# Two of a pair's weight sums by adding transfers, in six groups of a hybrid attention and convolution block

## The chip, the cores and the metric

The kernel runs on one core of a Trainium2 chip. The metric is the time of one execution on the device in microseconds (us); the number that counts is the median of several runs.

The core has five engines that work side by side and wait for each other by semaphores: PE (TensorE, the matrix engine, with its weight loads shown as PEld), DVE (VectorE), ACT (ScalarE), POOL (GpSimd) and SP (SyncE, which here only issues transfers). Sixteen DMA engines move data between the chip's main memory and the on-chip memory. A transfer is issued from the queue of an engine, here SP's and, for a few small ones, ACT's (q1 and q10 in the profile).

## The reference

One layer over 256 tokens of width 4096, all in float32:

```
xn   = rms_norm(x)
proj = xn @ w_in                 # 4096 x 14336: q, k, v, z_a, a_c, g_c, z_c, each 2048 wide
y_a  = rms_norm(chunked_attention(q, k, v, rel_table)) * silu(z_a)      # 16 heads of 128
y_c  = rms_norm(conv_module(a_c, g_c)) * silu(z_c)
h    = x + concat(y_a, y_c) @ w_out                                      # 4096 x 4096
gate = sigmoid(rms_norm(h) @ w_ple_gate + b)                             # 4096 x 4096
out  = rms_norm(h + gate * (p @ w_ple))
```

The conv module is `a * sigmoid(g)`, a causal depthwise convolution of 31 taps, a layer norm, a swish and a 2048 x 2048 product. Nearly all the work is in the products with the weights, which are read once each from main memory.

## The kernel before

**Products.** The 256 tokens are two halves of 128 rows. A weight tile is 128 rows of a weight matrix by two blocks of 512 columns (`two_columns`, L99; 512 KB). PE multiplies float32 numbers that are split in a high and a low part, so that each 128 x 128 by 128 x 512 product takes three matmuls (high by high, low by high, high by low; `add`, L365). To make the parts of a weight tile, `parts_of` (L199) has ACT write a rounded copy (L204, `wh`) and DVE subtract it from the tile (L205, `wl`).

**Pairs.** `mixed_product` (L327) makes two column blocks of a product at once. It goes over pairs of 128-row blocks of the contracted dimension, 16 pairs for 4096 rows, in an order that is written out by hand (L318 to L325). A pair is done in one of two ways. A plain pair makes the 8 block products as they are, 24 matmuls. A pair with a star is a seven: a Strassen-like scheme that makes 7 block products of sums, 21 matmuls. The sums on the side of the inputs (`comb`) are made once. Those on the side of the weights are made for each such pair, from its two weight tiles w0 and w1 (L421 to L432): `ua` holds w0[0] + w0[1] and w0[1] + w1[1], `ub` holds ua[0] + w1[1] and that plus w1[0]. These are four DVE additions of 128 x 512 (L426, L427, L430, L431), and `ua` and `ub` are split in their parts as the weight tiles are (`pair_parts`, L308; `uh`, `ul`). A seven so takes less of PE and more of DVE and ACT.

Four of the seven products go to PSUM banks of their own (the helpers P1, P5, P6, P7; L418), which are taken from the pool `ps_tmp` at a group's first seven and are read back after its last one (`on_helpers`, L455). Transposes and the attention use the same four banks.

**Groups.** In the first half of the kernel the calls of `mixed_product` through `scaled_pair` (L478) are eight groups: `glu_conv` (L689) for the pairs of column blocks a_c and g_c, c = 0 to 3, and `heads` (L883) for q and k, g = 0 to 3. They run as glu 0, glu 1, heads 0, glu 2, heads 1, glu 3, heads 2, heads 3. Each `heads` is followed by the product for v (`product`, L224) and by the attention of its four heads. Glu 0 has the order `first`, glu 3 the order `early_six` with six sevens, and the other six groups the order `early` with four sevens two apart:

```
early = units("1 3 5 7 0* 9 2* 11 4* 13 6* 15 8 10 12 14")
early_fills = (4, 6, 7, 1, 5, 1, 5, 1, 5, 1, 2, 4, 6, 6, 6, 4)
```

The convolution is work for DVE that is laid between the pairs: each group of `glu_conv` puts 124 taps (L671) into a queue (`later`), and after the n-th pair `fill` (L182) takes the n-th number of `early_fills` out of it. In heads 3 the layer norm and swish stand in that queue, four pieces after each pair.

**Buffers and order.** Weight tiles come from a pool with five buffers (`wpool`, tag w), their high and low parts from three each, `ua` and `ub` together from two (`upool`, tag u), `uh` and `ul` from two each. All loads of weight tiles are issued by SP (L403); a load waits until DVE has freed its buffer. The order of each engine's instructions is set when the program is made, by a planner that goes by program order, by the buffers and by its own estimates of durations; on the chip each engine goes through its list in that order and waits where something is late. Some places are pinned to program order. POOL has 19 instructions, among them the one memset of a part of each attention bias (L895), and issues no transfer.

Of the kernel before, what the change touches and what calls it, by code (L numbers as in the profile page):

```python
# [25 lines left out]
def hybrid_block(  # L26
# [23 lines left out]
    nc = tc.nc  # L50
# [32 lines left out]
    upool = pool("upool", 2, first_sums)  # L83
# [228 lines left out]

    def units(text):

        return [(int(u.rstrip("*")), u.endswith("*")) for u in text.split()]


    dense = units("1 0* 3 2* 5 4* 6* 7 8* 9 10* 11 12* 14* 13 15")  # L318
    first = units("0 1 3 5 7 9 11 13 15 2* 8 4* 10 6* 12 14")
    early = units("1 3 5 7 0* 9 2* 11 4* 13 6* 15 8 10 12 14")  # L320
    early_six = units("1 3 5 7 0* 9 2* 11 4* 13 6* 15 8* 10* 12 14")

    early_fills = (4, 6, 7, 1, 5, 1, 5, 1, 5, 1, 2, 4, 6, 6, 6, 4)
    final = units("1 0* 3 2* 5 4* 6* 7 8* 9 10* 12* 11 13 14 15")
    late = units("1 3 5 7 9 11 13 15 0* 2 4* 6 8* 10* 12 14")  # L325

    def mixed_product(  # L327
        w, col, lhs, comb, order, on_helpers, ahead=None, fills=(0,), on_begin=None, apart=NB,
# [53 lines left out]
        def add_plain(n, k, wh, wl, **kw):  # L382
            pair = order[n][0]
            for j in range(2):
                for h in range(NH):
                    name = (("P2", "P3"), ("P4", "X"))[h][j]
                    add(name, block(2 * pair + k, h), (wh[:, j], wl[:, j]), n, k == 1, **kw)

        done, after = 0, ExitStack()
        if begin:  # L390
            done, behind = begin(add_plain)
# [3 lines left out]
        for n, (pair, seven) in enumerate(order):  # L395
            if n < done:
                continue
            if ahead:
                ahead(pair)
            wts = []  # L400
            for k in range(2):
                wt = wpool.tile([P, 2, NB], F32, tag="w", name="wt")
                nc.sync.dma_start(wt, two_columns(w, 2 * pair + k, col, apart))  # L403
                wts.append(wt)
            if n >= len(order) - n_left:
                for k in range(2):
                    tiles = left[2 * (n - len(order) + n_left) + k]
                    held.append((2 * pair + k, parts_of(wts[k], 2, tiles and tiles())[0]))
                fill(fills[n % len(fills)])
                continue  # L410
            if not seven:
                for k in range(2):
                    add_plain(n, k, *parts_of(wts[k], 2)[0])
                fill(fills[n % len(fills)])
                continue
            begins = not helper
            if begins:
                for name in ("P1", "P5", "P7", "P6"):  # L418
                    helper[name] = ps_tmp.tile([P, NB], F32, tag="tmp", name=f"acc_{name}")
                banks.update(helper)  # L420
            w0, w1 = wts  # L421
            ua = upool.tile([P, 2, NB], F32, tag="u", name="ua")
            ub = upool.tile([P, 2, NB], F32, tag="u", name="ub")
            plus = partial(nc.vector.tensor_tensor, op=ALU.add)
            w0h, w0l = parts_of(w0, 1)[0]
            plus(ua[:, 0], w0[:, 0], w0[:, 1])  # L426
            plus(ua[:, 1], w0[:, 1], w1[:, 1])  # L427
            uah, ual = pair_parts(ua)
            w1h, w1l = parts_of(w1, 2)[0]
            plus(ub[:, 0], ua[:, 0], w1[:, 1])  # L430
            plus(ub[:, 1], ub[:, 0], w1[:, 0])  # L431
# [12 lines left out]
            add("P3", s_of(3), (w1h[:, 1], w1l[:, 1]), n, True)  # L444
            add("P6", s_of(2), (ubh[:, 0], ubl[:, 0]), n, True)
            add("P4", block(k1, 1), (ubh[:, 1], ubl[:, 1]), n, True)
            if begins and on_begin:
                on_begin()
            if begins:
                tc.add_manual_dep(  # L450
                    made[first].ins, last_transpose[0].ins.name,
                    mybir.DependencyInfo(mybir.DependencyClass.NoSync, mybir.DependencyReason.DATA),
                    reason="transposes before the helpers take their banks",
                )
            if n == last_seven:  # L455
                on_helpers(helper)
            fill(fills[n % len(fills)])
# [61 lines left out]
    r_x = cpool.tile([P, NH], F32, name="r_x")  # L519
# [169 lines left out]
    def glu_conv(c):  # L689
        if c == 0:  # L690
            sg, gate = scaled_pair(
                w_in0, o_a, o_g - o_a, first, r_x, (1,), begin=first_pairs
            )
        else:
            last = c == CW // NB - 1
            sg, gate = scaled_pair(
                w_in0, o_a + c * NB, o_g - o_a, early_six if last else early, r_x, early_fills,
                ahead=more_combinations if last else None,
            )
        for h in range(NH):  # L700
            nc.scalar.activation(gate[:, h, :], gate[:, h, :], AF.Sigmoid)
            tt(sg[:, h, :], sg[:, h, :], gate[:, h, :], ALU.mult)
        uT = spool.tile([P, 4, T], F32, tag="hd", name="uT", bufs=5)
        for pair in range(2):
            pt = tmp_psum()
            for i in range(2):
                for h in range(NH):
                    b = 2 * pair + i
                    nc.tensor.transpose(
                        pt[:, i * T + h * P : i * T + (h + 1) * P],  # L710
                        sg[:, h, b * P : (b + 1) * P],
                        ident,
                    )
# [557 lines left out]
```

## Time and profile before

| | |
|---|---|
| median of 3 runs | 2037.13 us (2036.65 to 2038.36) |
| the profiled execution | 2039.1 us |
| its span, from first to last instruction | 2037.3 us |
| matmuls of PE | 9106 |
| granted clock of PE, mean | 0.998 |
| read from main memory | 406.39 MB, 202 GB/s over the span |
| stretch of the six groups | about 99 to 859 us of the span |

The profile gives for each engine how long it was busy and what ended its idle time. A row of the groups of instructions names the line, the engine, the operation and the tiles (out<-in), how many there were, their busy time and mean duration, and the idle time just before them with what ended it. A row of the waits names who waited for whom, the total, the times and the longest. A row of the stretches has for each engine the busy time and, in brackets, the count of its instructions, then the granted clock, the busy share of the DMA engines and the rate. "Landing" is the time from the issue of a transfer to its last byte.

### The profile page before, as it was taken

Reading aid. Unit: us, or ns where it says so; the run is one execution under the profiler, and the core shown is the slowest. Engines: PE = TensorE matmul, PEld = TensorE weight load, DVE = VectorE, ACT = ScalarE, POOL = GpSimd, SP = SyncE. Lnnn points to the kernel's source line nnn. Section 1 sums busy time; section 2 is a strip of 40 time slices with the busy share of each in tenths; the row PEclk is TensorE's granted clock in tenths of the full one; section 3 lists DMA queues with packets and bytes.
Section 4 is the critical chain, followed back from the end, with each engine's and each line's share of the span. In section 5 each row is a group of like instructions: output and inputs, shape, how many; then the busy total and the mean of one; then the engine's idle time right before and its main releaser. Section 6 shows DMA issues by size and latency. Waiting matters only on the chain.

```text
span 2037.3 us, 26041 instructions
## 1 busy us (share of the span) xinstructions
PE 2019.6 (99%) x9106; PEld 1659.5 (81%) x9106; DVE 1887.9 (93%) x2688; ACT 1200.8 (59%) x1559; POOL 8.1 (0%) x19
## 2 busy tenths in 40 slices
PE   9999999999999999999999999999999999999997
PEld 7888888877888888888888888888888888888876
DVE  7999999799989998868899999999999999999998
ACT  7655546554565546676555656676565666655555
POOL 0000000000000000000000000000000000000000
PEclk9999999999999999999999999999999999999999
DMA  8666665666656665655666666676666656666765
GB/s 295 188 200 204 204 187 165 202 191 189 184 185 204 201 188 183 186 184 199 190 216 204 197 216 199 219 238 204 214 201 205 214 185 208 198 221 205 235 208 179
DMA packets 161853, 412.29 MB, mean 202 GB/s; under 512 B 12974, under 2 KB 16190, under 8 KB 161722
## 3 DMA queue, kind: packets, MB, share of 16 engines
q1 hardware_dynamic: 161072, 409.80, 63.3%
q8 instruction: 71, 1.16, 0.2%
q10 hardware_dynamic: 650, 0.84, 0.1%
q14 instruction: 60, 0.49, 0.1%
HBM read 406.39 MB, written 4.19 MB: 202 GB/s over the span
## 4 chain that ended last, share of the span: by engine, by line
PE 86%; DVE 10%; issue 2%; DMA 1%; ACT 1%; POOLq 0%; POOL 0%; ACTq 0%; DVEq 0%
PE acc L370 61%; PE acc_P L370 15%; PE acc L218 7%; DVE wl L205 4%; DVE cv L677 3%; DMA wt<-in_w_in_dram 1%; PE tmp_ps L170 1%; DVE ul L205 1%; PE tmp_ps L867 0%; PE tmp_ps L849 0%; ACT wh L204 0%; PE acc L358 0%; PE tmp_ps L834 0%; DVE z L492 0%; PE tmp_ps L872 0%
## 5 line engine op out<-in xcount | busy, mean ns | idle before, releaser
L370 PE MATMUL acc<-wh,big_t 128*128 128x512 f32 x3788 | 1172.1, 391 | 0.6 <-DVE z L988 0.3
L204 ACT CAST wh<-wt 128x1024 fp32r<-128x1024 f32 (+1 forms) x737 | 715.8, 982 | 543.0 <-PE acc L370 330.6
L205 DVE TENSOR_TENSOR wl<-wt,wh 128x1024 fp32r<-128x1024 f32 (+1 forms) x737 | 825.4, 1132 | 65.0 <-ACT wh L204 60.1
L370 PEld LDWEIGHTS acc<-wh,big_t 128*128 128x128 f32 x3788 | 708.4, 188 | 146.5 <-issue 0.6
L370 PE MATMUL acc<-wl,big_t 128*128 128x512 f32 x1894 | 731.1, 391 | 1.0 <-DVE wl L205 1.0
L370 PEld LDWEIGHTS acc<-wl,big_t 128*128 128x128 f32 x1894 | 355.2, 188 | 76.7 <-DVE wl L205 3.1
L677 DVE SCALAR_TENSOR_TENSOR cv<-uT,dw,cv 128x255 f32<-128x255 f32 (+23 forms) x480 | 204.9, 467 | 1.1
L204 ACT CAST uh<-ub 128x1024 fp32r<-128x1024 f32 x122 | 128.5, 1054 | 126.2 <-DVE ub L431 102.7
L218 PE MATMUL acc<-wh,big_t 128*128 128x512 f32 x560 | 173.1, 390 | 0.0
L204 ACT CAST uh<-ua 128x1024 fp32r<-128x1024 f32 x122 | 128.7, 1055 | 71.7 <-DVE ua L427 63.5
L205 DVE TENSOR_TENSOR ul<-ub,uh 128x1024 fp32r<-128x1024 f32 x122 | 149.0, 1221 | 8.8 <-ACT uh L204 7.8
L370 PE MATMUL acc_P<-uh,big_t 128*128 128x512 f32 x504 | 154.4, 392 | 0.0
L205 DVE TENSOR_TENSOR ul<-ua,uh 128x1024 fp32r<-128x1024 f32 x122 | 148.9, 1220 | 0.4 <-ACT uh L204 0.2
L218 PEld LDWEIGHTS acc<-wh,big_t 128*128 128x128 f32 x560 | 104.8, 188 | 21.4
L370 PEld LDWEIGHTS acc_P<-uh,big_t 128*128 128x128 f32 x504 | 93.3, 188 | 22.2 <-ACT uh L204 3.7
L218 PE MATMUL acc<-wl,big_t 128*128 128x512 f32 x280 | 109.1, 390 | 0.0
L426 DVE TENSOR_TENSOR ua<-wt 128x512 f32<-128x512 f32 x122 | 83.9, 688 | 25.9 <-DMA wt<-in_w_in_dram 19.0
L370 PE MATMUL acc_P<-ul,big_t 128*128 128x512 f32 x252 | 96.8, 392 | 0.0
L427 DVE TENSOR_TENSOR ua<-wt 128x512 f32<-128x512 f32 x122 | 83.7, 686 | 3.9 <-DMA wt<-in_w_in_dram 3.0
L431 DVE TENSOR_TENSOR ub<-ub,wt 128x512 f32<-128x512 f32 x122 | 83.8, 687 | 1.0
L430 DVE TENSOR_TENSOR ub<-ua,wt 128x512 f32<-128x512 f32 x122 | 83.7, 686 | 0.3
L370 PE MATMUL acc<-uh,big_t 128*128 128x512 f32 x244 | 75.4, 390 | 0.0
(241 smaller groups left out, 1523.0 us busy)
## 6 DMA issues: line engine op xcount, KB each, us to landing
wt<-in_w_in_dram SPq DMA_DIRECT2D x447, 512.0 KB, 4.0
wt<-in_w_out_dram SPq DMA_DIRECT2D x128, 512.0 KB, 4.2
wt<-in_w_ple_gate_dram SPq DMA_DIRECT2D x128, 512.0 KB, 4.2
wt<-in_w_pw_dram SPq DMA_DIRECT2D x32, 512.0 KB, 4.5
hc<-in_x_dram SPq DMA_DIRECT2D x8, 512.0 KB, 5.8
wt<-in_w_ple_dram SPq DMA_DIRECT2D x8, 512.0 KB, 4.2
xin<-in_x_dram SPq DMA_DIRECT2D x7, 512.0 KB, 8.2
out_dram<-hc SPq DMA_DIRECT2D x12, 256.0 KB, 2.4
```

The lines of the kernel that those rows point to most:

```text
L170: nc.tensor.transpose(pt[:, i * T + h * P : i * T + (h + 1) * P], src[:, h, b * P : (b + 1) * P], ident,)
L204: nc.scalar.copy(wh[:, :kc, :], wt[:, :kc, :]),
L205: nc.vector.tensor_tensor(wl[:, :kc, :], wt[:, :kc, :], wh[:, :kc, :].bitcast(F32), ALU.subtract),
L218: nc.tensor.matmul(acc, a, b[:, k, :], start=kb == 0 and kind == 0, stop=kb == kblocks - 1 and kind == 2,)
L370: nc.tensor.matmul(banks[name], a, b, start=name not in begun, stop=final and ends[name] == n and kind == 2 and not (left and name in "P2 ...
L426: plus(ua[:, 0], w0[:, 0], w0[:, 1])
L427: plus(ua[:, 1], w0[:, 1], w1[:, 1])
L430: plus(ub[:, 0], ua[:, 0], w1[:, 1])
L431: plus(ub[:, 1], ub[:, 0], w1[:, 0])
L677: nc.vector.scalar_tensor_tensor(cv[:, i, PAD - k :], uT[:, i, : T + k - PAD], dw[:, b, k : k + 1], cv[:, i, PAD - k :], ALU.mult, ALU.add,)
```

## The change

In the order `early`, and only there, the four sevens get a plus in place of the star and stand three apart in place of two: units 3, 6, 9 and 12 in place of 4, 6, 8 and 10. The numbers of taps laid between are set anew, with the same total of 64; glu 3 keeps its order and the old numbers under a new name.

For a pair with a plus the two sums in `ua` are made by transfers. A new function, `sums_ahead`, is called right after the weight tiles of a unit n are asked for, and for each plus unit among n, n + 1 and n + 2 that has none yet it takes a tile of tag u and issues two transfers of 512 KB: SP loads the column block w0[1] into both halves, and POOL then adds w0[0] to the first half and w1[1] to the second. DVE's additions at L426 and L427 fall away for these pairs. As w0[1] is needed for nothing else, the first weight tile of such a pair is loaded with one column block, 256 KB. `ub` is no tile of its own any more; the two additions left write over `ua`, once its parts are made.

```diff
-    early = units("1 3 5 7 0* 9 2* 11 4* 13 6* 15 8 10 12 14")
+    early = units("1 3 5 0+ 7 9 2+ 11 13 4+ 15 8 6+ 10 12 14")
...
-    early_fills = (4, 6, 7, 1, 5, 1, 5, 1, 5, 1, 2, 4, 6, 6, 6, 4)
+    early_fills = (5, 6, 1, 5, 6, 1, 5, 6, 1, 5, 6, 1, 2, 5, 5, 4)
+    six_fills = (4, 6, 7, 1, 5, 1, 5, 1, 5, 1, 2, 4, 6, 6, 6, 4)
...
+        sums = {}
+
+        def sums_ahead(n):
+            for m in range(n, min(n + 3, len(order))):
+                if order[m][1] != "+" or m in sums:
+                    continue
+                ua = sums[m] = upool.tile([P, 2, NB], F32, tag="u", name="ua")
+                rows = w[2 * order[m][0] * P : (2 * order[m][0] + 1) * P, :]
+                step = P * rows.ap[0][0]
+
+                def columns(first, step):
+                    return bass.AP(
+                        tensor=rows.tensor, offset=rows.offset + first,
+                        ap=[list(rows.ap[0]), [step, 2], [1, NB]],
+                    )
+
+                nc.sync.dma_start(ua, columns(col + apart, 0))
+                nc.gpsimd.dma_start(ua, columns(col, step + apart), accum_op=ALU.add)
...
-                nc.sync.dma_start(wt, two_columns(w, 2 * pair + k, col, apart))
+                if seven == "+" and k == 0:
+                    nc.sync.dma_start(wt[:, 0], w[2 * pair * P : (2 * pair + 1) * P, col : col + NB])
+                else:
+                    nc.sync.dma_start(wt, two_columns(w, 2 * pair + k, col, apart))
                 wts.append(wt)
+            sums_ahead(n)
...
             w0h, w0l = parts_of(w0, 1)[0]
-            plus(ua[:, 0], w0[:, 0], w0[:, 1])
-            plus(ua[:, 1], w0[:, 1], w1[:, 1])
+            if seven == "+":
+                ua = ub = sums[n]
+            else:
+                ua = upool.tile([P, 2, NB], F32, tag="u", name="ua")
+                plus(ua[:, 0], w0[:, 0], w0[:, 1])
+                plus(ua[:, 1], w0[:, 1], w1[:, 1])
             uah, ual = pair_parts(ua)
             w1h, w1l = parts_of(w1, 2)[0]
+            if seven != "+":
+                ub = upool.tile([P, 2, NB], F32, tag="u", name="ub")
             plus(ub[:, 0], ua[:, 0], w1[:, 1])
             plus(ub[:, 1], ub[:, 0], w1[:, 0])
```

More of the change, by code (lines that the diff above doesn't have):

```diff
@@ L313, in units @@
     def units(text):
-        return [(int(u.rstrip("*")), u.endswith("*")) for u in text.split()]
+        return [(int(u.rstrip("*+")), u[-1] if u[-1] in "*+" else "") for u in text.split()]
     dense = units("1 0* 3 2* 5 4* 6* 7 8* 9 10* 11 12* 14* 13 15")
     first = units("0 1 3 5 7 9 11 13 15 2* 8 4* 10 6* 12 14")
-    early = units("1 3 5 7 0* 9 2* 11 4* 13 6* 15 8 10 12 14")
+    early = units("1 3 5 0+ 7 9 2+ 11 13 4+ 15 8 6+ 10 12 14")
     early_six = units("1 3 5 7 0* 9 2* 11 4* 13 6* 15 8* 10* 12 14")
-    early_fills = (4, 6, 7, 1, 5, 1, 5, 1, 5, 1, 2, 4, 6, 6, 6, 4)
+    early_fills = (5, 6, 1, 5, 6, 1, 5, 6, 1, 5, 6, 1, 2, 5, 5, 4)
+    six_fills = (4, 6, 7, 1, 5, 1, 5, 1, 5, 1, 2, 4, 6, 6, 6, 4)
     final = units("1 0* 3 2* 5 4* 6* 7 8* 9 10* 12* 11 13 14 15")
@@ L421, in mixed_product @@
             w0, w1 = wts
-            ua = upool.tile([P, 2, NB], F32, tag="u", name="ua")
-            ub = upool.tile([P, 2, NB], F32, tag="u", name="ub")
             plus = partial(nc.vector.tensor_tensor, op=ALU.add)
             w0h, w0l = parts_of(w0, 1)[0]
-            plus(ua[:, 0], w0[:, 0], w0[:, 1])
-            plus(ua[:, 1], w0[:, 1], w1[:, 1])
+            if seven == "+":
[4 more added lines that the diff above has]
+                plus(ua[:, 1], w0[:, 1], w1[:, 1])
             uah, ual = pair_parts(ua)
             w1h, w1l = parts_of(w1, 2)[0]
+            if seven != "+":
+                ub = upool.tile([P, 2, NB], F32, tag="u", name="ub")
             plus(ub[:, 0], ua[:, 0], w1[:, 1])
@@ L696, in glu_conv @@
             sg, gate = scaled_pair(
-                w_in0, o_a + c * NB, o_g - o_a, early_six if last else early, r_x, early_fills,
+                w_in0, o_a + c * NB, o_g - o_a, *((early_six, r_x, six_fills) if last else (early, r_x, early_fills)),
                 ahead=more_combinations if last else None,
```

## The prediction

> **What bounds the kernel now.** I read the busy shares and the chain on the page first, then the stretches of the six groups that the diff touches, then what waits in them.
>
> ```profile
> span 2037.3 us, 26041 instructions
> ...
> PE 2019.6 (99%) x9106; PEld 1659.5 (81%) x9106; DVE 1887.9 (93%) x2688; ACT 1200.8 (59%) x1559; POOL 8.1 (0%) x19
> ...
> DMA  8666665666656665655666666676666656666765
> GB/s 295 188 200 204 204 187 165 202 191 189 184 185 204 201 188 183 186 184 199 190 216 204 197 216 199 219 238 204 214 201 205 214 185 208 198 221 205 235 208 179
> ...
> PE 86%; DVE 10%; issue 2%; DMA 1%; ACT 1%; POOLq 0%; POOL 0%; ACTq 0%; DVEq 0%
> ...
> L426 DVE TENSOR_TENSOR ua<-wt 128x512 f32<-128x512 f32 x122 | 83.9, 688 | 25.9 <-DMA wt<-in_w_in_dram 19.0
> ...
> L427 DVE TENSOR_TENSOR ua<-wt 128x512 f32<-128x512 f32 x122 | 83.7, 686 | 3.9 <-DMA wt<-in_w_in_dram 3.0
> ...
> wt<-in_w_in_dram SPq DMA_DIRECT2D x447, 512.0 KB, 4.0
> ```
>
> PE is busy 99% of the span and holds 86% of the chain. A busy share can hide slow matmuls, so I checked the pace where PE is fed without a break: in the chain of waits, a stretch of 192 matmuls takes 43.55 us.
>
> ```profile
> 499.47 43.55 PE acc L218 x192
> ```
>
> That is 0.2268 us each. An early group is 12 plain pairs of 24 matmuls and 4 sevens of 21, 372 in all: 84.4 us at that pace. The sums by stretch hold the six groups with what lies beside them (glu 1 and heads 0; glu 2 and heads 1; heads 2; heads 3; the v products and part of the attention lie outside).
>
> ```profile
> core 0: us, PE busy (x) PEld busy (x) DVE busy (x) ACT busy (x) POOL busy (x), PEclk, DMA share, GB/s
> 99.50:271.50 172.00, 171.88 (x768) 140.90 (x767) 171.40 (x273) 89.78 (x101) 0.31 (x1) 1.00 0.64 199
> 325.00:498.50 173.50, 170.58 (x767) 138.90 (x766) 156.53 (x239) 92.47 (x118) 0.31 (x1) 1.00 0.62 190
> 634.00:722.00 88.00, 87.79 (x395) 71.91 (x394) 87.61 (x140) 47.43 (x53) 0.31 (x1) 1.00 0.63 197
> 772.00:859.00 87.00, 87.00 (x404) 71.42 (x403) 74.41 (x106) 52.95 (x76) 0.70 (x1) 1.00 0.59 182
> ```
>
> The reader is to see two things. DVE is as full as PE in the first and third row (171.40 of 172.00, 87.61 of 88.00). And PE at a granted clock of 1.00 still lacks only 0.12, 2.92, 0.21 and 0.00 us. A full engine beside a full PE is no loss unless PE waits for it, so the waits decide. These are from the waits of heads 1, heads 2, glu 1 and heads 0 in turn (us in total, times, longest).
>
> ```profile
> ACT uh L204 <- DVE ub L431: 13.4, 4, 4.0
> ...
> DVE ua L426 <- DMA wt<-in_w_in_dram: 2.8, 2, 2.5
> ...
> PEld tmp_ps L834 <- DVE z L492: 2.2, 2, 1.7
> PEld acc L370 <- DVE wl L205: 2.0, 3, 1.2
> ...
> PE tmp_ps L834 <- DVE z L492: 1.6, 2, 1.2
> PE acc L370 <- DVE wl L205: 1.0, 2, 0.8
> ```
> ```profile
> PEld acc_P L370 <- DVE ul L205: 0.9, 2, 0.6
> ...
> PEld tmp_ps L834 <- DVE z L492: 0.2, 1, 0.2
> PE acc_P L370 <- DVE ul L205: 0.2, 1, 0.2
> ```
> ```profile
> PEld acc_P L370 <- DVE ul L205: 1.2, 4, 0.6
> ...
> PEld acc L370 <- DVE z L492: 0.2, 1, 0.2
> PEld tmp_ps L709 <- DVE z L702: 0.2, 1, 0.2
> ```
> ```profile
> PEld tmp_ps L834 <- DVE z L492: 0.3, 1, 0.3
> ```
>
> PE waits for DVE 1.6 + 1.0 + 0.2 = 2.8 us in the six groups. The weight loads, which run ahead of the matmuls, wait for it 2.2 + 2.0 + 0.9 + 0.2 + 1.2 + 0.2 + 0.2 + 0.3 = 7.2 us. What a freer DVE can give lies between these two sums and nothing.
>
> **The change part by part.** *The two adds go.* 24 units (4 in each of 6 groups) lose L426 and L427: 24 x (0.688 + 0.686) = 33.0 us of DVE time, 5.5 us a group. The matmuls stay as they are, 372 a group, so PE's 84.4 us stay too. DVE's work is off the path except where PE waits for it. I take all 2.8 us of those waits as gone, because 5.5 us a group is more than each group's wait; the ends are 0 (the order moves the waits elsewhere) and 7.2 us. What is late next is PE itself.
>
> *One weight load halves, two transfers come.* The first tile of such a pair loads one column (256 KB less), SP issues a load of the sum tile (512 KB) and POOL an adding transfer (512 KB): 768 KB more, 24 times. Per group that is 4 x 786,432 B = 3.15 MB in 86 us, 37 GB/s on top of the 199 of the first row; if adding also reads the tile back, 4 x 0.52 MB = 24 more. The sum, 236 to 260 GB/s, lies under the 295 that the page's first slice carried, so on average it fits. It costs nothing on the path as long as loads land in time; the cover is the five weight buffers, and the bounds are in the rivals below. SP's issues, 24 more of 0.37 us (the next fence), are nothing beside some 2.7 us from load to load.
>
> *A new wait.* The cast of the sum (ACT) and its subtraction (DVE) now wait for the adding transfer, not for DVE. Behind that cast stand the casts of the next weight tiles, and behind those PE. How early is it issued? The loads of heads 1, with their landing:
>
> ```profile
> L403 SPq DMA_DIRECT2D wt<-in_w_in_dram x19: 367/368/368, 410.3 to 459.1; - x19
> ...
> DMA to landing us min/median/max: 3.6/4.0/8.2
> ```
>
> 18 steps in 48.8 us are 2.71 us a load. The sum of unit m is issued behind the second load of unit m - 2, which is 3 loads ahead of unit m's first; and a load is issued some 5 buffers ahead of its cast. So the lead is about 8 x 2.71 = 21.7 us. The chain in it: the sum tile's load, then POOL's own issue, then the adding transfer. For the load I take 4.0 us. POOL's issue of a transfer is not in the trace; its only instruction in the groups is a memset, and landing of the four bias transfers of the same 512 KB is the widest row.
>
> ```profile
> L895 POOL MEMSET bias<- x4: 306/306/307, 193.4 to 767.6; 64x256 f32 x4
> ...
> DMA to landing us min/median/max: 4.9/5.9/9.0
> ```
>
> So the chain is at least 3.6 + 0.3 + 3.6 = 7.5 us, and at most 9.0 + 9.0 for the load and POOL's issue together with a slow landing, and 9.0 more if the adding reads its target as a second transfer: 27 us. I take 4.0 + 1 + 8.0 = 13 us, nearest to the plain loads, with POOL's issue at three times its memset and the read back counted as a second landing. 13 is under 21.7, so the wait is hidden. If that cover is gone, ACT still has some: it waited for DVE up to 4.0 us at a time in heads 1 (13.4 us in 4 times) where PE waited 2.8 - 0.2 = 2.6 us in all for DVE.
>
> *Sevens three apart, from unit 3 to unit 12.* A plain pair is 24 x 0.2268 = 5.44 us of PE, a seven 4.76. The first seven comes 5.4 us earlier and takes the four spare PSUM banks from the attention before it; the last one ends 2 x 5.44 = 10.9 us later. Tightest is heads 3:
>
> ```profile
> L876 ACT ACTIVATE y_a<-tmp_ps,den x7: 358/360/370, 771.8 to 786.7; 128x128 f32<-128x128 f32 x7
> ```
> ```profile
> L370 PE MATMUL acc_P<-wh,big_t x8: 389/389/389, 794.2 to 825.1; 128*128 128x512 f32 x8
> ```
> ```profile
> L746 PE MATMUL tmp_ps<-lnsum,mean_w x2: 379/431/483, 827.0 to 827.3; 128*128 128x256 f32 x2
> ```
> ```profile
> L803 DVE TENSOR_TENSOR big_t<-cv,big_t x16: 416/418/420, 876.4 to 884.8; 128x256 fp32r<-128x256 f32 x16
> ```
> ```profile
> 904.12 0.58 PE L370 MATMUL acc<-wh,big_t 128*128 128x512 f32 x1
> ```
>
> The attention's last read of a bank starts at 786.7; the first seven would start at 794.2 - 5.4 = 788.8: it fits, by under 2 us. The layer norm's mean (L746) gets its bank when the helpers give it back at 827, so the layer norm moves 10.9 us: its last split ends at 885.2 + 10.9 = 896, ahead of the product that reads it at 904.1. Both cost nothing, the first with little cover. At the end of each group three plain units (16.3 us) stand behind the last seven in place of five; in them DVE has 6 subtractions, 16 taps and the helper sums, all closer to the group's end than before, which is why I don't count the whole 7.2 us.
>
> The sum: the profiled execution took 2039.1 us with a span of 2037.3; 2037.3 - 2.8 = 2034.5, 2036.3 in its own time. The runs' median is 2037.13, which is 2.0 under that execution. So 2037.1 - 2.8 = **2034.3 us**.
>
> **Rivals.** *Crowded loads* (slower). The adding transfer and the load of the sum tile share the 16 DMA engines with the weight loads. The trace has one like it: the bias load in heads 1. There a weight tile came late, DVE stood 2.5 us and PE then waited 1.0 us for L205. The other three bias loads cost no such wait. If one unit in four pays as that one did, 24 / 4 x 1.0 = 6 us: 2037.1 - 2.8 + 6 = 2040; if each pays, 2058. It decides once a landing passes the 8.2 us of heads 1. The Trainium skill ("DMA: Bandwidth & Descriptors", section "Queues, rings and completion order") says that a DMA engine switches between queues only after a whole packet, 9 to 17 descriptors; by that an adding transfer would hold a weight load up by its full share of an engine, not by half. No row of before shows it, as almost all bytes are in one queue. By the rule the price is the 2058 of each unit paying, without it the 2034.3.
>
> *Late sums* (slower). If the chain takes its upper 27 us, it passes the lead by 5.3 us; less the 4.0 that ACT can stand, 1.3 us reach PE in each unit: 24 x 1.3 = 31, so 2068 with no gain kept. It decides from a chain of about 25.7 us; up to there it only eats the gain. For it: nothing in the trace bounds an adding transfer. Against it: three landings in a row must each be as slow as the slowest quoted. A price between, 0.5 us a unit, gives 2049.
>
> *Nothing moves.* The planner orders DVE anew; waits of 2.8 us in 520 can come back elsewhere. Then the time is 2037.1, within 1 us. This is also the time if DVE's fullness was never the cause: heads 0 has a DVE busy to the brim and no PE wait at all.
>
> *All weight-load waits go*: 2037.1 - 7.2 = 2029.9.
>
> **How the numbers follow.** Forecast (2032 to 2036.5) 0.39, nothing moves 0.15, crowded loads 0.25, late sums 0.20, all weight-load waits 0.01. The range runs from the full 7.2 us, 2030, to the 2058 of crowding in each unit; past it lies about half of late sums and little else, 0.12. The bound of 0.2%, about what a measurement of this kernel can tell from no change, is 4.1 us: 2033.0 and 2041.2. Of the forecast, 0.08 lies under 2033.0, since the mean of 2.8 and 7.2 would do; with the last rival, faster 0.09. Same: 0.31 of the forecast, 0.15, and 0.06 of crowding at one unit in four: 0.52. Slower: 0.19 + 0.20 = 0.39. The likeliest case's own range is 2032 to 2036.5.
>
> **What would show it.** Right: L426 and L427 at x98 with DVE's busy time near 1855 us; PE's waits for DVE in the six groups under 1 us; no wait of ACT's cast of ua for the adding transfer that PE shares; landing of weight loads with a median under 5 us. Crowding: DVE or ACT waiting for wt at more than the page's 19.0 + 3.0 us. Late sums: ACT waiting for ua, then PE for L204 or L205, 24 times alike. The forecast is wrong if the adding transfer's landing is far over 8 us, or if PE's total at the same count of matmuls doesn't fall by some 2 us.

## The result, and the profile after

The changed kernel takes 2067.14 us, the median of 4 runs (2066.96 to 2067.59), against 2037.38 us of the kernel before on the same chip (2036.65 to 2038.36). The ratio is 1.0144, with a 95% interval of 1.0128 to 1.016: some 30 us slower, where 2034.3 was forecast. The profiled execution took 2066.96 us.

These are rows of the page of the changed kernel that answer to those shown of the kernel before. L452 and L453 are the old L426 and L427, L406 and L407 are the two transfers of a sum, and q0 is the queue of POOL's adding transfers.

```profile
span 2065.2 us, 26124 instructions
...
PE 2028.9 (98%) x9106; PEld 1664.8 (81%) x9106; DVE 1861.9 (90%) x2640; ACT 1198.7 (58%) x1559; POOL 37.5 (2%) x43
...
q0 software_dynamic: 6528, 12.58, 3.8%
...
L371 PE MATMUL acc<-wl,big_t 128*128 128x512 f32 x1894 | 735.6, 394 | 9.2 <-DVE wl L205 9.0
...
L452 DVE TENSOR_TENSOR ua<-wt 128x512 f32<-128x512 f32 x98 | 67.4, 688 | 18.6 <-DMA wt<-in_w_in_dram 14.8
...
L453 DVE TENSOR_TENSOR ua<-wt 128x512 f32<-128x512 f32 x98 | 67.4, 687 | 1.9 <-DMA wt<-in_w_in_dram 1.2
...
wt<-in_w_in_dram SPq DMA_DIRECT2D x423, 512.0 KB, 4.2
...
ua<-in_w_in_dram SPq DMA_DIRECT2D x24, 512.0 KB, 5.0
ua<-in_w_in_dram POOLq DMA_DIRECT2D x24, 512.0 KB, 8.0
```

The change did what it says: 24 fewer of each addition, and DVE 1887.9 - 1861.9 = 26.0 us freer. But PE, with the same 9106 matmuls, is busy 9.3 us longer and the span is 27.9 us longer. So PE both waits more and runs slower at times. The waits of the stretch of the six groups (95 to 900 us; us in total, times, longest) name two new ones, at L458 and for a transferred sum, and what PE then stands for:

```profile
DVE ua L458 <- DMA wt<-in_w_in_dram: 25.0, 14, 4.0
...
ACT uh L204 <- DMA ua<-in_w_in_dram: 16.3, 2, 10.0
...
PE acc L371 <- DVE wl L205: 9.0, 11, 2.8
...
PE acc L371 <- ACT wh L204: 8.7, 3, 5.2
```

ACT stands only twice for a transferred sum, but for 16.3 us, and PE then stands 8.7 us for the casts behind it. DVE stands 14 times, 25.0 us, for a weight tile at L458, the first addition that is left in a plus unit. Before, PE's waits for DVE in the six groups came to 2.8 us, and it stood for no cast (L204) there.

Where the time went is told by the length of each group, from the end of DVE's last read-back of one group's sums (the `z<-acc` of L520, the old L492) to that of the next, against the kernel before (worked out from the traces, us):

| kernel | glu 0 | glu 1 | heads 0 | glu 2 | heads 1 | glu 3 | heads 2 | heads 3 | rest |
|---|---|---|---|---|---|---|---|---|---|
| after | 4.8 | -0.9 | 7.1 | 1.2 | 2.2 | 7.9 | -1.2 | 7.1 | -0.3 |
| e1, order only | 0.1 | -1.6 | 1.3 | -0.3 | -1.2 | -0.1 | 0.7 | 6.0 | -0.1 |
| e4, no adding transfer | 0.6 | -1.8 | 2.9 | -0.7 | -1.2 | -0.4 | -1.5 | 5.5 | 0.3 |
| e7, heads 3 as before | 5.3 | -1.8 | 5.9 | 1.9 | 1.3 | 8.0 | -1.5 | 0.8 | 1.0 |
| e13, casts in order | 0.9 | -1.3 | 0.9 | -0.4 | -3.6 | -0.3 | -1.4 | 5.7 | -0.2 |
| e14, e13 with heads 3 as before | 0.6 | -1.3 | 0.8 | -0.4 | -3.6 | -0.3 | -1.3 | 0.9 | -0.4 |

Glu 0 and glu 3 have no pair with a plus. They lose 4.8 and 7.9 us because the first sum of the group behind each (glu 1, heads 2) is already loaded in them, and ACT comes to its cast before DVE has read them back. PE stands twice:

```profile
102.52 0.70 PE L371 MATMUL acc<-wh,big_t 128*128 128x512 f32 x2 [3.30 <-ACT wh L204]
650.18 1.22 PE L371 MATMUL acc<-wh,big_t 128*128 128x512 f32 x2 [5.21 <-ACT wh L204]
```

ACT's own list at the first of the two places (start, duration; in brackets the idle time before and what ended it):

```profile
90.91 1.05 ACT L204 CAST wh<-wt 128x1024 fp32r<-128x1024 f32 x1
98.27 1.05 ACT L204 CAST uh<-ua 128x1024 fp32r<-128x1024 f32 x1 [6.31 <-DMA ua<-in_w_in_dram]
99.22 1.04 ACT L204 CAST wh<-wt 128x1024 fp32r<-128x1024 f32 x1
```

The transfers of this sum and the next, with durations and the first and last start, are from the rows of the tile `ua` between 82 and 106 us:

```profile
L406 SPq DMA_DIRECT2D ua<-in_w_in_dram x2: 368/370/372, 83.7 to 86.0; - x2
L407 POOL DMA_DIRECT2D ua<-in_w_in_dram x2: 1232/1300/1369, 89.5 to 98.5; - x2
```

The chain from the load's issue to the cast is 98.27 - 83.7 = 14.6 us, close to the 13 of the forecast; over all 24 sums the add landed 11.3 to 18.5 us after the load's issue (worked out from the trace). But ACT was through with what stands ahead of the cast at 90.91 + 1.05 = 91.96, only 8.3 us after that issue, and all later casts of weight tiles wait behind it. The second place is alike: the cast stands 9.98 us and starts at 646.30, 14.8 us after its load's issue at 631.5.

```profile
635.26 1.06 ACT L204 CAST wh<-wt 128x1024 fp32r<-128x1024 f32 x1 [0.34 <-PE acc L371]
646.30 1.04 ACT L204 CAST uh<-ua 128x1024 fp32r<-128x1024 f32 x1 [9.98 <-DMA ua<-in_w_in_dram]
```

### The profile page after: what moved, and what is told of

Read it like the earlier page. It is cut to its first block, busy times and chain, and to the rows that moved or that the text cites. A ratio compares the mean times of both kernels' runs of the same rounds, so it can differ in the third digit from the quotient of the medians.

```text
span 2065.2 us, 26124 instructions
## 1 busy us (share of the span) xinstructions
PE 2028.9 (98%) x9106; PEld 1664.8 (81%) x9106; DVE 1861.9 (90%) x2640; ACT 1198.7 (58%) x1559; POOL 37.5 (2%) x43
## 4 chain that ended last, share of the span: by engine, by line
PE 64%; DVE 2%; issue 1%; ACT 1%; DMA 1%; POOLq 0%; POOL 0%; ACTq 0%; DVEq 0%
PE acc L371 45%; PE acc_P L371 12%; PE acc L218 5%; DVE wl L205 1%; PE tmp_ps L170 1%; DMA wt<-in_w_in_dram 1%; ACT wh L204 0%; PE acc L359 0%; ACT uh L204 0%; PE tmp_ps L862 0%; DVE ul L205 0%; PE tmp_ps L877 0%; DVE ub L458 0%; PE tmp_ps L895 0%; DVE ub L459 0%
## 5 line engine op out<-in xcount | busy, mean ns | idle before, releaser
L204 ACT CAST wh<-wt 128x1024 fp32r<-128x1024 f32 (+1 forms) x737 | 714.0, 980 | 562.8 <-PE acc L371 345.6
L205 DVE TENSOR_TENSOR wl<-wt,wh 128x1024 fp32r<-128x1024 f32 (+1 forms) x737 | 826.0, 1134 | 88.0 <-ACT wh L204 82.7
L204 ACT CAST uh<-ua 128x1024 fp32r<-128x1024 f32 x146 | 153.7, 1053 | 109.0 <-DVE ua L453 41.3
L705 DVE SCALAR_TENSOR_TENSOR cv<-uT,dw,cv 128x230 f32<-128x230 f32 (+24 forms) x480 | 203.4, 471 | 1.2
L205 DVE TENSOR_TENSOR ul<-ua,uh 128x1024 fp32r<-128x1024 f32 x146 | 178.4, 1222 | 18.1 <-ACT uh L204 17.5
L204 ACT CAST uh<-ub 128x1024 fp32r<-128x1024 f32 x98 | 103.1, 1052 | 93.1 <-DVE ub L459 74.3
L205 DVE TENSOR_TENSOR ul<-ub,uh 128x1024 fp32r<-128x1024 f32 x98 | 119.8, 1222 | 7.1 <-ACT uh L204 6.1
L452 DVE TENSOR_TENSOR ua<-wt 128x512 f32<-128x512 f32 x98 | 67.4, 688 | 18.6 <-DMA wt<-in_w_in_dram 14.8
L371 PE MATMUL acc_P<-wh,big_t 128*128 128x512 f32 x244 | 75.4, 390 | 0.0
L453 DVE TENSOR_TENSOR ua<-wt 128x512 f32<-128x512 f32 x98 | 67.4, 687 | 1.9 <-DMA wt<-in_w_in_dram 1.2
L459 DVE TENSOR_TENSOR ub<-ub,wt 128x512 f32<-128x512 f32 x98 | 67.4, 688 | 1.0
```

What stands on the lines that cost most here:

```text
L204: nc.scalar.copy(wh[:, :kc, :], wt[:, :kc, :]),
L205: nc.vector.tensor_tensor(wl[:, :kc, :], wt[:, :kc, :], wh[:, :kc, :].bitcast(F32), ALU.subtract),
L371: nc.tensor.matmul(banks[name], a, b, start=name not in begun, stop=final and ends[name] == n and kind == 2 and not (left and name in "P2 ...
L705: nc.vector.scalar_tensor_tensor(cv[:, i, PAD - k :], uT[:, i, : T + k - PAD], dw[:, b, k : k + 1], cv[:, i, PAD - k :], ALU.mult, ALU.add,)
```

## The experiments

All numbers are medians beside the kernel before on the same chip. The theory to be tested has three parts: (1) late sums, since ACT comes to the cast too early; (2) weights held up by the adding transfers; (3) heads 3, by its order alone. The rivals: each part could be an effect of another, or of the spacing.

### e1_order_only: the order and the taps, all sums by DVE

```diff
-    early = units("1 3 5 0+ 7 9 2+ 11 13 4+ 15 8 6+ 10 12 14")
+    early = units("1 3 5 0* 7 9 2* 11 13 4* 15 8 6* 10 12 14")
```

> The changed order and tap numbers (sevens at units 3, 6, 9, 12) with all sums made by DVE as before; no new transfer. If the transfers are the whole cause (held loads and late sums), about 2037 us, within 3 us of the kernel before. If the moved order is part of it (heads 3 ended 7.1 us later in the changed kernel than its start explains, with the layer norm's mean 35 us later), 2044 us or more, and heads 3 still has PE's wait of about 3 us near its end.

Measured: 2045.72 us, ratio 1.0033 (1.002 to 1.0045). Almost all of it, 6.0 us, is in heads 3. The rows of its stretches there (us, busy time and count of each engine, granted clock, share of the DMA engines, GB/s), and of the layer norm's mean:

```profile
846.00:851.00 5.00, 2.69 (x12) 1.88 (x10) 4.93 (x10) 4.40 (x6) 0.00 (x0) 1.00 0.00 0
851.00:855.50 4.50, 3.98 (x10) 3.18 (x11) 4.50 (x6) 1.53 (x2) 0.00 (x0) 0.62 0.63 181
```
```profile
L774 PE MATMUL tmp_ps<-lnsum,mean_w x2: 379/431/483, 838.0 to 838.3; 128*128 128x256 f32 x2
```
```profile
847.62 1.08 DVE L786 TENSOR_TENSOR cv<-cv,mu 128x256 f32<-128x256 f32 x3
848.77 1.23 DVE L794 TENSOR_TENSOR sq<-sq 128x1024 f32<-128x1024 f32 x1
849.92 0.42 DVE L786 TENSOR_TENSOR cv<-cv,mu 128x256 f32<-128x256 f32 x1
850.25 2.35 DVE L205 TENSOR_TENSOR wl<-wt,wh 128x1024 fp32r<-128x1024 f32 x2
```

The mean starts at 838.0 where it was 827.0, 11.0 us later, about the 10.9 that were foreseen. What was not foreseen: the layer norm's work is now in DVE's list ahead of the subtractions for the last products, which start at 850.25, with no transfers moving at all from 846 to 851. DVE comes to them 12.3 us after the mean starts; in the kernel before it was at 834.44, 7.4 us after it:

```profile
833.44 1.09 DVE L758 TENSOR_TENSOR cv<-cv,mu 128x256 f32<-128x256 f32 x3
834.44 2.35 DVE L205 TENSOR_TENSOR wl<-wt,wh 128x1024 fp32r<-128x1024 f32 x2
```

PE stands 2.83 us for L205 at 851.5, and the granted clock of the stretch from 851 to 855.5 is 0.62.

### e7_heads3_stars: heads 3 with the order and the sums of before

```diff
+    early_stars = units("1 3 5 7 0* 9 2* 11 4* 13 6* 15 8 10 12 14")
...
-            q, k = scaled_pair(w_in0, o_q + g * NB, o_k - o_q, early, r_x,
+            q, k = scaled_pair(w_in0, o_q + g * NB, o_k - o_q, early_stars if g == n_g - 1 else early, r_x,
```

> As changed in five groups; heads 3 has the order and the DVE sums of the kernel before. If the late layer norm in heads 3 costs what the order alone lost there (6.0 us), 2067.1 - 7 = 2060 us, and PE's wait of 3.0 us near the end of heads 3 is gone. If the loss there came from its transfers alone, the same time; the two are told apart by the run with the order alone, which had that wait without a transfer.

Measured: 2060.6 us, ratio 1.01 (1.0085 to 1.0115). Heads 3 falls from 7.1 to 0.8 us, the other groups stay. Part 3 is a cost by itself, and it is the order's.

### e2_two_apart: the transferred sums in the old places

```diff
+    early = units("1 3 5 7 0+ 9 2+ 11 4+ 13 6+ 15 8 10 12 14")
...
+    early_fills = (4, 6, 7, 1, 5, 1, 5, 1, 5, 1, 2, 4, 6, 6, 6, 4)
```

> The transfers at the old places (units 4, 6, 8, 10, old tap numbers). If each adding transfer costs by holding the loads, the cost per unit is at least the same and two apart leaves 10 us in place of 16 for it: 2065 to 2085 us. If the place of the sevens was the cause, it falls to 2050 us or less.

Measured: 2053.97 us, ratio 1.0071 (1.0056 to 1.0086). Glu 0 and glu 3 lose 6.5 and 7.1 us again, heads 3 only 1.2. Its waits in the same stretch:

```profile
ACT uh L204 <- DMA ua<-in_w_in_dram: 27.6, 10, 10.0
```

So part 1 comes with the transfers, not with the order. The time lies between the two that were expected, some 13 us under the changed kernel with as many adding transfers: DVE's wait at L458 is 2.5 us here in place of 25.0, so part 2 hangs on the order and the fillers too.

### e4_no_add and e5_plain_pool: the adding transfer left out, or without its adding

```diff
-                nc.gpsimd.dma_start(ua, columns(col, step + apart), accum_op=ALU.add)
```
```diff
-                nc.gpsimd.dma_start(ua, columns(col, step + apart), accum_op=ALU.add)
+                nc.gpsimd.dma_start(ua, columns(col, step + apart))
```

In e4 the sums hold w0[1] alone; in e5 POOL's transfer overwrites it.

> As changed, without POOL's adding transfers: the sum tiles hold w0[1] alone, so the sums are wrong; SP's load of the tile and the order stay. If the adding transfers are the cause (late and holding the loads), 2036 to 2042 us and DVE's waits for wt at L457 or so under 8 us in all (25.0 in the changed kernel). If the extra load or the order is, 2055 us or more.

> As changed, but POOL's transfer writes over the tile and adds nothing (so the sums are wrong); its issue, queue and bytes from main memory are the same. If it is the adding that holds the loads (3.5 us of the DMA engines for 512 KB, packets of 178 ns where a load's take 83), the engines are held 1.4 us, the landing falls from 8.0 to 5 us or less and the time to about 2048 us. If it is the software queue as such, the time stays within 5 us of 2067.

Measured: e4 2041.52 us, ratio 1.0012 (1.0002 to 1.0021); e5 2057.34 us, ratio 1.0087 (1.0072 to 1.0102). The waits of e4, then of e5, and e5's transfers by issue:

```profile
DVE ua L457 <- DMA wt<-in_w_in_dram: 8.1, 13, 1.5
...
ACT uh L204 <- DMA ua<-in_w_in_dram: 2.7, 1, 2.7
```
```profile
DVE ua L458 <- DMA wt<-in_w_in_dram: 16.3, 16, 2.2
...
ACT uh L204 <- DMA ua<-in_w_in_dram: 12.4, 2, 8.2
```
```profile
ua<-in_w_in_dram POOLq DMA_DIRECT2D x24, 512.0 KB, 5.2
```

L457 is L458 of the changed kernel. Without POOL's transfer only heads 3 (5.5 us) and heads 0 (2.9) still lose; the other groups stand between -1.8 and 0.6. A plain transfer from POOL's queue lands after 5.2 us where the adding one takes 8.0, and by the ratios it costs some 15 us (1.0087 - 1.0012) of the some 27 (1.0144 - 1.0012) that the adding one does. So more than half of the cost comes with POOL's transfer whether it adds or not; its adding makes that longer.

### e3_behind_stars and e9_own_tiles: is it the buffers?

e3 leaves the first two sums of glu 1 and heads 2 to DVE. e9 keeps them transferred, but takes their tiles from another pool (tag act), so that they should wait for no buffer of `ua`.

```diff
+    early_two = units("1 3 5 0* 7 9 2* 11 13 4+ 15 8 6+ 10 12 14")
```
```diff
-                ua = sums[m] = upool.tile([P, 2, NB], F32, tag="u", name="ua")
+                ua = sums[m] = (act if len(sums) < borrow else upool).tile([P, 2, NB], F32, tag="act" if len(sums) < borrow else "u", name="ua")
```

> As changed, but in glu 1 and heads 2, the two groups behind a group of stars, the first two sevens have their sums made by DVE; 20 adding transfers in place of 24. Late sums at these two starts (ACT waited 6.3 and 10.0 us for them, glu 0 and glu 3 end 4.8 and 7.9 us later): about 2067.1 - 12.7 = 2054 us, and no wait of ACT for ua over 2 us. Held loads at an even price per transfer: 2067.1 - 4 x 29.8 / 24 = 2062 us.

> As changed, but in glu 1 and heads 2 the first two sums get tiles of another pool (tag act), so that their loads need not wait for the stars of the group before to give back ua and ub. If the sums are late there because of the buffers, ACT's waits for the transfers (6.3 and 10.0 us) go, and with them 4.8 and 7.9 us: about 2054 us. If they are late because the transfer itself is slow, within 4 us of 2067.

Measured: e3 2067.23 us, ratio 1.0134 (1.0119 to 1.0149); e9 2070.2 us, ratio 1.0147 (1.013 to 1.0164). The waits of e3, then of e9:

```profile
ACT uh L204 <- DMA ua<-in_w_in_dram: 19.2, 2, 10.9
```
```profile
ACT uh L204 <- DMA ua<-in_w_in_dram: 19.6, 2, 9.9
```

Glu 0 and glu 3 are cured in both (1.3 and -0.4 us; 0.4 and -0.2), but glu 1 and heads 2 now lose 4.0 and 7.7, and 6.7 and 7.1. The stall moves on, into the group itself, but it is not the same stall. In e3 the load of the first sum of glu 1 starts at 130.40, when DVE's subtraction of a star's `ua` ends (129.15 + 1.22) and gives a buffer back; the load of its own unit's first tile follows 2.5 us later. In e9 the two sums of glu 1 in tiles of `ua`'s pool (told apart by what each load waits for) are loaded first, at 83.5 and 85.8, and the first one in another tile only at 103.88, 20 us later than the first sum of the changed kernel. Its add lands at 121.00, and the cast waits for it though it stands right behind a cast of one column block, that is in its unit's own place:

```profile
110.69 0.62 ACT L204 CAST wh<-wt 128x512 fp32r<-128x512 f32 x1 [1.62 <-DVE wl L205]
121.02 1.04 ACT L204 CAST uh<-ua 128x1024 fp32r<-128x1024 f32 x1 [9.71 <-DMA ua<-in_w_in_dram]
```

So in both the transfer starts too late, which costs as much as a cast that comes too early. Neither run shows that buffers have no part in the changed kernel's stalls.

### e8_split_add: the adding transfer in two of 256 KB

```diff
-                nc.gpsimd.dma_start(ua, columns(col, step + apart), accum_op=ALU.add)
+                for j in range(2):
+                    nc.gpsimd.dma_start(ua[:, j], columns(col, step + apart)[:, j], accum_op=ALU.add)
```

> As changed, but each adding transfer is made of two of 256 KB, one for each half of the tile. If a DMA engine serves the other queue only after its whole share of the adding transfer, loads get a turn between the halves, are held 1.8 us in place of 3.5, and DVE's waits for wt at L459 halve (25.0 us): about 2062 us. If the second half must wait for the first to land, the sums are later still, and where they are late already (glu 1, heads 2) the time rises: 2070 us or more.

Measured: 2066.58 us, ratio 1.013 (1.0115 to 1.0145), DVE's wait for weights at L458 (here L459) 22.9 us against 25.0. Inconclusive: each half still takes 6.5 us to land, and nothing else moved.

### e13_casts_in_order: ACT casts a transferred sum behind its unit's first block

The edit orders two instructions of ACT and adds no wait on the chip. ACT's list is otherwise left to the planner, which also orders parts of DVE's and SP's lists anew.

```diff
-            w0h, w0l = parts_of(w0, 1)[0]
+            (w0h, w0l), w0_made = parts_of(w0, 1)
...
-            uah, ual = pair_parts(ua)
+            uah, ual = pair_parts(ua, w0_made[0] if seven == "+" else None)
...
+        parts, made = parts_of(src, 2, tiles)
+        (behind and tc.add_manual_dep(made[0].ins, behind.ins.name, mybir.DependencyInfo(mybir.DependencyClass.NoSync, mybir.DependencyReason.DATA), reason="in order")); return parts
```

> The changed kernel with one edge more: on ScalarE the cast of a transferred sum (uh<-ua, L204) may not stand ahead of the cast of its own unit's first block (wh<-wt). Nothing else is altered, and the transfers are issued as in the changed kernel. Theory A (late sums come from where the cast stands: it was put some eight casts ahead, behind no full buffer, so ScalarE sits at it for 6.3 and 10.0 us while the adding transfer is under way, and all later casts wait behind it): ScalarE's waits for ua, 16.3 us in all in the changed kernel, fall under 3 us, the two groups before glu1 and heads 2 lose their 12.7 us, and the time is about 2067.1 - 12.7 = 2054. Theory B (the sums are late for the matmuls themselves, wherever the cast stands): PE waits for uh in the plus unit instead, and the time stays within 3 us of 2067. Theory C (only moved: the waits go to other first plus units, as in the two runs that took stars or other buffers): 2064 to 2070 with the waits in other groups.

Measured: 2038.72 us (10 runs), ratio 1.0006 (0.9996 to 1.0015). That is 28.4 us under the changed kernel, more than twice the 12.7 expected for part 1; the only loss left is heads 3. ACT's list at the same place, and the transfers of the first two sums:

```profile
111.27 0.62 ACT L204 CAST wh<-wt 128x512 fp32r<-128x512 f32 x1 [1.62 <-DVE wl L205]
111.80 1.04 ACT L204 CAST uh<-ua 128x1024 fp32r<-128x1024 f32 x1
```
```profile
L406 SPq DMA_DIRECT2D ua<-in_w_in_dram x2: 368/368/368, 84.1 to 86.4; - x2
L407 POOL DMA_DIRECT2D ua<-in_w_in_dram x2: 1232/1300/1369, 89.3 to 98.9; - x2
```

The first two transfers start within 0.4 us of where they did; the cast is not asked for until 111.80, 27.7 us behind the load's issue, and nobody waits for it. And the waits for weights at L458 are gone too; of the new kind of PE's waits only the one of heads 3 is left:

```profile
DVE ua L452 <- DMA wt<-in_w_in_dram: 5.2, 4, 1.6
...
PE acc L371 <- DVE wl L205: 2.8, 1, 2.8
```

So part 2 is no cost of its own with this order: as many adding transfers run and their landing is no shorter (median 8.3 us), but the additions left in a plus unit no longer stand for a weight tile behind them. What stands is L452, for glu 3's six stars, 5.2 us (6.0 in the changed kernel). Why L458 no longer stands is in the issue of the loads (worked out from the traces, 24 units each): in the changed kernel the second weight tile of a plus unit is issued 3.0 to 6.1 us before DVE is free for L458, in e13 10.3 to 17.9 us. The planner moved these loads together with the casts, so the 28.4 us are the gain of both; which part of the new lists moved the loads was not tried.

### e14_casts_h3, e12_order_five, e16_star_casts: the gain, and what makes it

e14 is e13 with heads 3 as in e7. e12 has e14's order, but all sums by DVE; e16 is e12 with the order of casts of e13 for its first sums.

```diff
-    early = units("1 3 5 0+ 7 9 2+ 11 13 4+ 15 8 6+ 10 12 14")
+    early = units("1 3 5 0* 7 9 2* 11 13 4* 15 8 6* 10 12 14")
+    early_stars = units("1 3 5 7 0* 9 2* 11 4* 13 6* 15 8 10 12 14")
```

> The same edge, and heads 3 with the order and the sums of the kernel before. Theory A: 2067.1 - 12.7 - about 6.5 (what heads 3 alone gave back) = 2048; what is then left over the kernel before, some 9 us, is loads held behind the adding transfers. Theory B or C: 2060, as with heads 3 alone.

> No transferred sums: VectorE adds all sums as before, but in the five groups other than heads 3 the sevens stand three apart with the changed kernel's fillers. By the theory that the order costs something only in heads 3 (its late layer norm, 6.0 us of the 6.4 of the run with the order alone), the other five groups keep their -0.1 to -1.6 us: 2036 to 2040 against 2039.3 before, so within 0.2%, perhaps a shade faster. If the order costs elsewhere too: over 2042.

> The kernel with five groups reordered and all sums by VectorE (2037.2), with the cast of the first sum behind its unit's first cast in those five groups. No transfers, so it differs from the run at 2034.6 by the transferred sums alone. If the edit matters only because a transferred sum comes late: no change, 2036 to 2038.5, and the transferred sums are worth the 2 to 3 us between this and 2034.6. If the edit is a gain of its own: 2034 to 2035, and the transferred sums are worth nothing.

Measured: e14 2034.61 us (10 runs), ratio 0.9984 (0.9975 to 0.9993); e12 2037.18 us, ratio 0.9997 (0.9988 to 1.0006); e16 2037.44 us against 2039.19, ratio 0.9993 (0.9984 to 1.0002). Rows of e14's page:

```profile
span 2032.3 us, 26108 instructions
...
PE 2017.4 (99%) x9106; PEld 1660.4 (82%) x9106; DVE 1867.4 (92%) x2648; ACT 1199.1 (59%) x1559; POOL 32.7 (2%) x39
...
L372 PE MATMUL acc<-wl,big_t 128*128 128x512 f32 x1894 | 731.2, 391 | 0.0
```

PE's product with `wl` waits for nobody any more. e14 beats both kernels: 2.6 us under the kernel before, by an interval that leaves out 1. Neither the order (e12) nor the order of casts (e16) is a gain that can be told from none, so the transferred sums are what is left for it: 2.6 us from e12 to e14 on the same chip, though the intervals of the two ratios overlap a little.

### e17_two_apart_casts: is the spacing needed?

The edit of e13 on e2.

> The run with transferred sums in the old places and fillers, sevens two apart (2054.0), with the cast of the transferred sum behind its unit's first cast. If the place of the cast was the whole of its loss, the time falls to 2036 to 2039, and the spacing of three buys nothing. If a sum two units nearer still lands late for its unit (lead of three units of the order issues with no more than two plain units between), ScalarE and PE wait in every plus unit: 2042 to 2056.

Measured: 2051.62 us, ratio 1.0067 (1.0054 to 1.008). Glu 0 and glu 3 are cured (1.0 and -0.2 us against 6.5 and 7.1), but the loss is spread over other groups (4.4 in heads 0, 3.4 in heads 2):

```profile
ACT uh L204 <- DMA ua<-in_w_in_dram: 29.7, 10, 5.4
```

With one plain pair between sevens the sum lands too late even for its own turn, ten times: ACT comes to these casts 9.2 to 15.1 us after the load's issue, and the adds land 13.4 to 15.4 us after it. The spacing of three is needed as well.

### e15_unread_adds: transfers that nobody waits for

e12 with the load and the adding transfer of e14, into tiles of another pool that nobody reads.

```diff
-                ua = sums[m] = upool.tile([P, 2, NB], F32, tag="u", name="ua")
+                ua = sums[m] = act.tile([P, 2, NB], F32, tag="act", name="ux")
```

> The previous kernel of this call plus, at the places where the changed kernel issues them, the SyncE load and the adding transfer into tiles that nobody reads (twenty pairs of them, 512 KB each; the tiles come from the pool of larger activations). No engine waits for such a tile, the output is the reference's. Theory H (an adding transfer holds all other loads while its packets run, about 3.5 us each, and in a full stretch that makes weights late): 5 to 10 us over the run with five groups reordered, that is 2043 to 2048, with VectorE and ScalarE waiting for wt while adding transfers run. Rival (only the wait for the sums themselves costs): the same as that run within 1.5 us.

Measured: 2057.94 us, ratio 1.01 (1.0086 to 1.0114), 20.8 us over e12, far over what either theory gave. But it tests something else than meant: the load of such a tile waits until an earlier adding transfer into its buffer has landed, and that wait is SP's. SP's waits between 640 and 690 us, at its worst place (11.1 us lost in heads 2):

```profile
SPq L407 <- DMA ux<-in_w_in_dram: 15.3, 2, 7.7
```

Behind it in SP's queue stand the weight loads. So this run shows, at this place, the price of a waiting load ahead of other loads; the price of holding alone it doesn't show.

## Why the prediction was wrong

*The two adds go: right.* DVE lost 26.0 us of busy time against 33.0 of additions counted one by one (records of neighbours overlap a little, as the rows of e1 show: 1.23 us from 848.77, and the next at 849.92), and the waits of PE for DVE can go, as e14 shows. Its 2034.61 us, 2.6 under its kernel before, are close to the 2034.3 of the sum. The 2.8 us were sized well, but they are the gain of another kernel, with 20 such sums and heads 3 as before.

*A new wait: this step failed.* It was put as "13 is under 21.7, so the wait is hidden". The chain was right (14.6 and 14.8 us measured). The lead was not: it was counted from the loads to the unit's turn, as if the cast stood at its unit's turn in ACT's list. In the trace ACT came to it 8.3 us after the load's issue in glu 0 and 646.30 - 9.98 - 631.5 = 4.8 us in glu 3. Between the loads the lead was there: that of the first sum of glu 1 is issued at 83.7, that of its unit's own first weight tile at 105.5, 21.8 us later. In the kernel before a sum's early place in ACT's list cost little: ACT stood for DVE's sums up to 4.0 us at a time, and PE 2.8 us in all. e13 gives the cast the lead that was taken, 27.7 us for the first, and ACT's two stalls and the 12.7 us of glu 0 and glu 3 go. That the cast's place is the cause of these is shown; why the planner put it there was not tried.

*Transfers cost nothing as long as loads land in time: right with its condition, which was broken.* The cover was put as the five weight buffers, but the second weight tile of a plus unit is issued only 3.0 to 6.1 us ahead of L458. In e4, with 3.0 to 5.9 us and no adding transfer, that costs 8.1 us of waits; here the adding transfers hold loads up besides, and it is 25.0. Two stretches of the changed kernel, while one runs and right behind it:

```profile
227.00:230.50 3.50, 3.50 (x17) 2.88 (x17) 3.50 (x4) 0.52 (x1) 0.00 (x0) 1.00 0.79 120
231.00:234.50 3.50, 3.50 (x17) 2.92 (x16) 1.40 (x3) 0.03 (x1) 0.00 (x0) 1.00 1.05 397
```

The rate is 120 GB/s, then 397. The trace has no packet of the load queue from 227.0 to 230.5, though a load was issued at 227.23; it landed 5.8 us later, and DVE's L458 stood 2.1 us for it. The Trainium skill ("DMA: Bandwidth & Descriptors", section "Queues, rings and completion order") says that a DMA engine drains a whole packet of one queue before it turns to the next. This stretch agrees: the 256 packets of 2 KB that are the adding transfer, 16 for each DMA engine if they are spread evenly, run from 227.7 to 231.2, with 25 of the load queue near their end. Others are mixed: from 142.9 to 148.9 an adding transfer runs beside 615 packets of the load queue. The rival at 2058 was priced for this. Yet in e13, with the same transfers, L458 stands for nothing, since the loads are issued 10.3 us ahead or more. The early casts are not what DVE stands behind there: L458's waits lie in heads 0, glu 2, heads 1 and heads 3, and none in glu 1 and heads 2, where ACT comes too early.

*Heads 3: wrong in its price.* "Costs nothing" was argued from the layer norm's own reader at 904.1. The mean moved 11.0 us, much as foreseen, but what was late is the subtractions that stand behind the layer norm in DVE's list: 6.0 us (e1) and 6.3 (e7 against after).

The sum, with what the runs give: 4.8 + 7.9 = 12.7 us in glu 0 and glu 3 and 8.4 in the other five groups, both gone with the casts in order, 7.1 in heads 3, -0.3 in the rest: 27.9 us of span. The rival of late sums had the right engine, and by chance the right time (2068); its condition, a chain of 25.7 us in every unit, did not hold: the longest was 18.5. At that wait two units in 24 paid, with 10 us at most, and the casts behind them. In the other groups PE stood for DVE's subtractions, 9.0 us in 11 times, 2.8 of it in heads 3; that the rest of it, and the 8.4 us, come from DVE's waits at L458 is argued from their going together in e13.

## What to carry to other kernels

The lead of a transfer ends where the first instruction that waits for it stands in its engine's list, not where its result is used: read that place from the trace (the end of the instruction ahead of it), and count all that stands behind it. It begins where the transfer is really issued, which in e3 was when a buffer came free. When a sum is moved from an engine to a transfer, the order of its reader is part of the change. A step that is moved later is checked not only at its own reader but at each other instruction that now stands behind it in the same list.

## What the runs showed of the hardware

PE's clock fell after most stalls of 3 us or more, but not after all. The first two rows are the changed kernel behind the two casts of the sums, the third is heads 3:

```profile
102.50:107.50 5.00, 4.99 (x16) 3.92 (x17) 5.00 (x7) 3.03 (x4) 0.00 (x0) 0.66 0.75 206
650.00:657.00 7.00, 6.78 (x16) 4.91 (x17) 5.41 (x7) 3.32 (x5) 0.00 (x0) 0.53 0.76 203
874.50:879.00 4.50, 4.18 (x11) 3.31 (x12) 4.50 (x6) 1.33 (x2) 0.00 (x0) 0.62 0.61 185
```

At a granted clock of 0.53, 6.78 us of matmuls are worth 3.6; in the other rows 4.99 are worth 3.3 and 4.18 are worth 2.6. So each such stall cost 1.6 to 3.2 us on top of itself, 6.5 in all, most of the 9.3 us that PE is busy longer at the same count. The Trainium skill ("TensorE: Matmul & The Clock Gate", section "Part 1: The HAM clock gate") has the clock halved after an idle window of about 3.4 us; in e1 a stall of 2.83 us was followed by it. In e7 one of 3.66 us (to 102.99) was not: the granted clock from 102.9 to 109.9 is 1.00. So the runs show no sharp bound.

An adding transfer of 512 KB keeps POOL busy 1.2 us for its issue and lands after 8.0 us at the median, a plain one from the same queue after 5.2 (e5), a load from SP's queue after 4.2.
